# Scan step sizes made beside the grouped heads' values, differential values 512 columns wide

## The chip, the core and the metric

The kernel runs on one core of a Trainium2 chip as one program. The metric is the device time of one execution in microseconds; a run's time is that of its one core. TensorE (PE in the profile) multiplies, VectorE (DVE) and ScalarE (ACT) do the elementwise work, GpSimd (POOL) and SyncE (SP) issue transfers from their own queues. Matmuls accumulate into PSUM, eight banks of 512 float32 columns on each of 128 partitions.

## The reference, cut to what matters

Two layers of a hybrid trunk over 256 context tokens and 256 latent tokens of 1024 channels. In each layer one input projection feeds a bidirectional state-space scan, grouped-query attention (8 query heads, 2 heads of keys and values) and differential attention (8 heads); a gated merge, a layer norm and a gated feed-forward follow. Three parts of that projection matter here, with their widths:

```
p = split(h @ w_in)        # h: 512 tokens x 1024 channels
dt = softplus(p.dt + dt_bias)          # 64 columns: step sizes, 32 heads in 2 directions
a_dt = dt * -exp(a_log)                # decays of the scan, summed along the tokens
v_gqa  = p.gv                          # 256 columns: values of the 2 grouped heads
v_diff = p.dv                          # 1024 columns: values of the 8 differential heads, 128 each
o_head = softmax(...) @ v_head         # both attentions
```

## The kernel before

The program is not written in the order in which it runs. `trunk` records every operation in a plan; `Plan.schedule` (a list scheduler, `round` at line 346) then orders the operations of all engines at once, from a priority, a price for each operation (`cost`, line 208) and the room in SBUF and PSUM, and emits that order. So each instruction's place follows from the whole plan, every instruction has the same source line (586; 585 in the changed kernel), and the trace is read by tile names: `w` holds weights, `s` and `shared` are 2 KB work tiles (whole or shared by smaller ones), `ps` a PSUM bank, `cst` and `id` constants.

Every large product is exact float32 made from three reduced-precision terms: an operand is cast to float32r (`wh`, on ScalarE) and the rest is subtracted (`wl`, on VectorE); `mm3` (line 692) multiplies high by high, high by low and low by high into one bank:

```
T.matmul(ps, ah, bh, start=start, stop=False)
T.matmul(ps, ah, bl, start=False, stop=False)
T.matmul(ps, al, bh, start=False, stop=stop)
```

`proj` (line 931) makes 128 output channels of the projection with `dense`: weights stationary, the tokens `xT` moving, 8 channel blocks x 3 terms = 24 matmuls of 512 tokens. The first `HALVES` = 7 products of a layer over all tokens are cut into two halves of 256 tokens (context, latent), 48 matmuls, so that the context half can begin before the latent tokens are ready. In layer 0 some products begin when only half of the channels is modulated (`early_terms`, line 883).

Values are made the other way round, tokens on the partitions: the tokens are stationary, the weights move. `values` (line 1174) makes 256 columns for the 4 blocks of 128 tokens, two blocks to a PSUM bank one after the other: 4 x 8 x 3 = 96 matmuls of 256 columns. It is called once a layer for the grouped heads (`O_GV`, within `gqa_steps`, after the first key head) and four times for the differential heads (`O_DV`, `diff_steps`, one call for two heads).

The step sizes (`do_dt`, line 952) are a `proj` of 64 columns. Their softplus is computed with heads on the partitions, context in the upper and latent tokens in the lower half; four transposes bring steps and decays to tokens on partitions; matmuls with triangular constants make the running sums that the scan (`ssm_steps`) reads.

The scan's stream is interleaved with the attention and merge streams (`side`) by recorded TensorE cost: `advance` moves `side` on by `RATIO[i]` = 1.52 or 1.42 times what the scan's steps brought. Weights come in loads of 512 KB through SP's queue into 15 slots. Products with many terms take a bank from a share of six of the eight (`psd`, `CAP["d"]`).

## Time and profile before

| | |
|---|---|
| median of 3 runs | 2346.48 us (2346.24 to 2348.11) |
| the profiled execution, first to last instruction | 2345.3 us |
| TensorE busy | 2301.0 us, 98% |
| VectorE, ScalarE busy | 1670.1 us (71%), 1422.4 us (61%) |
| TensorE's mean granted clock | 0.993 |

The profiled execution's own span is 1.2 us under the median of the runs. Busy time of TensorE is a union of modelled spans, so the pace of a kind of matmul is read below from the start of one run of equal matmuls to the start of what follows.

### The profile page before, as it was taken

The numbers are of one execution on the slowest core, as the hardware profiler recorded it, in microseconds if no ns is written. First come the engines' busy times: TensorE is split into PE (matmuls) and PEld (weight loads), VectorE is DVE, ScalarE is ACT, GpSimd is POOL, SyncE is SP. The second block draws the span as 40 slices with busy tenths as digits, with TensorE's granted clock in tenths as the row PEclk, the third lists the DMA queues.
The fourth block names the chain that finished last, engine by engine and source line by source line (L and its number), as shares of the span: only waits on it lengthen the run. The fifth ranks groups of instructions, "written<-read, shape, count | busy, mean of one in ns | idle before, by whom it ended". The sixth has DMA issues, their size and how long they took to land. (4 is left out here: it accounts for less than half of the span.)

```text
span 2345.3 us, 38903 instructions
## 1 busy us (share of the span) xinstructions
PE 2301.0 (98%) x14423; PEld 1940.3 (83%) x14423; DVE 1670.1 (71%) x3438; ACT 1422.4 (61%) x2887; POOL 135.1 (6%) x216
## 2 busy tenths in 40 slices
PE   8999999999999999999999999999999999999998
PEld 4877777887887788898777778989988798998997
DVE  3889857888988864476333337999698888767655
ACT  4778745867767753345323235888586676646554
POOL 3102102000100100000000000001010100000000
PEclk9999999999999999999999999999999999999998
DMA  9746544332433465576555425527443345798662
GB/s 332 214 135 175 181 132 135 102 112 72 133 104 98 133 216 175 184 219 213 171 163 168 139 74 151 150 76 217 132 129 114 105 126 164 214 274 240 191 188 66
DMA packets 520702, 370.37 MB, mean 158 GB/s; under 512 B 20706, under 2 KB 472674, under 8 KB 520512
## 3 DMA queue, kind: packets, MB, share of 16 engines
q1 hardware_dynamic: 507296, 329.63, 47.3%
q0 software_dynamic: 13216, 38.25, 5.5%
q8 instruction: 113, 1.85, 0.3%
q14 instruction: 77, 0.63, 0.1%
HBM read 334.00 MB, written 33.82 MB: 157 GB/s over the span
## 5 line engine op out<-in xcount | busy, mean ns | idle before, releaser
L586 PE MATMUL ps<-s,w 128*128 128x512 f32 (+2 forms) x7608 | 1524.0, 355 | 8.2 <-DVE s L586 4.6
L586 PEld LDWEIGHTS ps<-s,w 128*128 128x128 f32 (+1 forms) x7608 | 1236.0, 189 | 237.1 <-issue 28.8
L586 ACT CAST w<-w 128x1024 fp32r<-128x1024 f32 (+2 forms) x486 | 454.4, 944 | 486.3 <-DVE w L586 256.8
L586 DVE TENSOR_TENSOR w<-w,w 128x1024 fp32r<-128x1024 f32 (+2 forms) x486 | 528.0, 1092 | 299.8 <-PE ps L586 203.0
L586 PE MATMUL ps<-shared,w 128*128 128x256 f32 x2544 | 313.2, 283 | 0.0
L586 PE MATMUL ps<-s,s 128*64 128x128 f32 (+6 forms) x2320 | 303.2, 361 | 7.6 <-DVE s L586 2.1
L586 PEld LDWEIGHTS ps<-shared,w 128*128 128x128 f32 x2544 | 308.5, 192 | 0.5 <-issue 0.3
L586 ACT ACTIVATE s<-s 128x512 f32<-128x512 f32 x424 | 260.6, 630 | 31.0 <-DVE s L586 24.7
L586 PEld LDWEIGHTS ps<-s,s 128*64 128x64 f32 (+3 forms) x2320 | 186.9, 152 | 90.6 <-issue 31.9
L586 DVE TENSOR_TENSOR s<-s,s 128x512 f32<-128x512 f32 (+2 forms) x298 | 196.2, 674 | 36.7 <-ACT s L586 34.5
L586 DVE TENSOR_TENSOR s<-s,ps 128x512 f32<-128x512 f32 x116 | 79.1, 684 | 133.3 <-PE ps L586 65.7
L586 DVE SCALAR_TENSOR_TENSOR s<-ps,misc,s 128x510 f32<-128x510 f32 (+2 forms) x188 | 139.3, 741 | 13.9 <-ACT s L586 11.8
L586 PE MATMUL ps<-w,s 128*128 128x256 f32 x960 | 119.7, 284 | 0.0
L586 PEld LDWEIGHTS ps<-w,s 128*128 128x128 f32 x960 | 117.2, 192 | 2.2 <-issue 1.5
L586 DVE TENSOR_TENSOR shared<-shared,shared 128x256 f32<-128x256 f32 (+2 forms) x241 | 97.2, 417 | 24.4 <-ACT shared L586 22.6
L586 DVE TENSOR_TENSOR s<-ps,s 128x256 fp32r<-128x256 f32 (+1 forms) x204 | 85.6, 444 | 30.4 <-ACT s L586 25.7
L586 ACT ACTIVATE shared<-shared 128x256 f32<-128x256 f32 x232 | 92.4, 416 | 23.4 <-DVE shared L586 20.7
L586 ACT CAST s<-ps 128x256 fp32r<-128x256 f32 (+1 forms) x204 | 74.4, 396 | 36.0 <-PE ps L586 32.1
L586 ACT ACTIVATE s<-ps,misc 128x512 f32<-128x512 f32 x68 | 50.6, 744 | 73.2 <-PE ps L586 73.0
L586 POOL DMA_DIRECT2D s<-dram x96 | 71.9, 753 | 375.0 <-PE ps L586 274.7
L586 ACT ACTIVATE s<-ps,tiny 128x512 f32<-128x512 f32 x112 | 76.7, 689 | 26.5 <-DVE tiny L586 18.9
L586 DVE SCALAR_TENSOR_TENSOR shared<-ps,misc,shared 128x256 f32<-128x256 f32 (+2 forms) x144 | 67.2, 478 | 29.4 <-PE ps L586 20.4
(102 smaller groups left out, 1512.5 us busy)
## 6 DMA issues: line engine op xcount, KB each, us to landing
w<-in_w_in_dram SPq DMA_DIRECT2D x200, 512.0 KB, 4.0
s<-in_ada_w_dram SPq DMA_DIRECT2D x192, 256.0 KB, 4.9
w<-in_ffn_w_in_dram SPq DMA_DIRECT2D x88, 512.0 KB, 3.9
s<-dram POOLq DMA_DIRECT2D x96, 256.0 KB, 5.6
s<-dram SPq DMA_DIRECT2D x64, 256.0 KB, 4.1
w<-in_w_ssm_out_dram SPq DMA_DIRECT2D x32, 512.0 KB, 4.1
w<-in_ffn_w_out_dram SPq DMA_DIRECT2D x32, 512.0 KB, 3.9
shared<-dram SPq DMA_DIRECT2D x112, 128.0 KB, 3.9
```

The lines of the kernel that those rows point to most:

```text
L586: getattr(attr[op.eng], fn)(*[real(v) for v in args], **{a: real(v) for a, v in kw.items()})
```

## The change

The 64 step-size columns are appended to the 256 columns of the grouped heads' values: `shared_values` moves 320 columns past each stationary token block, one bank for each of the 4 token blocks. These values are recorded ahead of all streams of a layer (in layer 0 their first half within `early_terms`), and `do_dt` reads columns 256 to 320 of the four banks, tokens already on partitions; its own projection, the copies into halves and the four transposes are gone, and bias and decay are loaded as rows broadcast to all partitions. `values` makes 512 columns (four heads) in a call for the differential heads, twice a layer, one bank a token block. `value_terms` goes through the channels two blocks at a time and, for each pair, through all four banks, which stay open until the last pair. The planner's price of a float32r matmul is now columns / 2.4 + m / 9.6 ns, m being the stationary operand's columns; it was max(columns / 2.4, 107) + 2.5 ns. Lines that only lose a comment are left out here.

```diff
-                return max(n / 2.4 if n >= 256 else 4 * n / 2.4, 107) + 2.5
+                return (n if n >= 256 else 4 * n) / 2.4 + m / 9.6
...
     def load_scalars(i):
-        na = tiny(2)
-        for r in (0, 64):
-            G.dma_start(out=na[r:r + 64, 0:1], in_=a_log[i].rearrange("t h -> (t h)").unsqueeze(1))
-            G.dma_start(out=na[r:r + 64, 1:2], in_=dt_bias[i].rearrange("t h -> (t h)").unsqueeze(1))
-        A.activation(na[:, 0:1], na[:, 0:1], AF.Exp)
+        na = th().rearrange("p (a c) -> p a c", c=64)
+        for m, src in enumerate((a_log, dt_bias)):
+            G.dma_start(out=na[:, m, :], in_=src[i].rearrange("t h -> (t h)").unsqueeze(0).to_broadcast([128, 64]))
+        A.activation(na[:, 0, :], na[:, 0, :], AF.Exp)
+        V.tensor_scalar(na[:, 0, :], na[:, 0, :], -1.0, None, ALU.mult)
...
-    def value_terms(pss, ws, blocks=range(4), have=()):
-        for t in blocks:
-            o = pss[t // 2][:, (t % 2) * 256:(t % 2) * 256 + 256]
-            ts_ = slice(t * 128, t * 128 + 128)
-            for k0, (wh, wl) in ws.items():
-                if k0 == 0 and t in have:
-                    continue
-                for k in range(k0, k0 + 4):
-                    mm3(o, xT[k][0][:, ts_], xT[k][1][:, ts_], wh[:, k - k0, :], wl[:, k - k0, :],
-                        k == 0, k == KT - 1)
+        n = sum(a.shape[-1] for a in src)
+        raw = plan.tile("w4", [128, len(ks), n], F32, "raw", CAP["raw"])
+        c = 0
+        for a in src:
+            w = a.shape[-1]
+            rows = a[ks[0] * 128:(ks[-1] + 1) * 128].rearrange("(k p) c -> p k c", p=128)
+            S.dma_start(out=raw[:, :, c:c + w], in_=rows)
+            c += w
+        wh = plan.tile("w4", [128, len(ks), n], F32R, "wh", CAP["wh"])
+        wl = plan.tile("w4", [128, len(ks), n], F32R, "wl", CAP["wl"])
+        A.copy(wh, raw)
+        V.tensor_sub(wl, raw, wh.bitcast(F32))
+        return wh, wl
+    def value_terms(pss, src, k0, k1):
+        n = sum(a.shape[-1] for a in src)
+            wh, wl = load_values(src, (k, k + 1))
+            for t in range(4):
+                ts_ = slice(t * 128, t * 128 + 128)
+                for d in range(2):
+                    mm3(pss[t][:, 0:n], xT[k + d][0][:, ts_], xT[k + d][1][:, ts_], wh[:, d, :], wl[:, d, :],
+                        k + d == 0, k + d == KT - 1)
     def load_x(q):
...
+    def shared_values(W):
+        return [W[:, O_GV:O_GV + 256], W[:, O_DT:O_DT + 64]]
     def early_terms():
...
-        for key in EARLY:
-            if key == O_GV:
-                w = load_w(W[0:512, key:key + 256], 4, 256)
-                early[0, key] = ([psd(), psd()], w)
-                value_terms(early[0, key][0], {0: w}, (0, 2))
-            else:
-                cols = 64 if key == O_DT else 128
-                w = load_w(W[:, key:key + cols], KT, cols, 32 if key == O_GK else 0)
-                early[0, key] = (psd(), w)
-                dense(early[0, key][0][0:cols], w, KT, xcols(0, NT), cols=cols, ks=range(4))
+        early[0, O_GV] = [psd() for _ in range(4)]
+        value_terms(early[0, O_GV], shared_values(W), 0, 4)
+        w = load_w(W[:, O_GK:O_GK + 128], KT, 128, 32)
+        early[0, O_GK] = (psd(), w)
+        dense(early[0, O_GK][0], w, KT, xcols(0, NT), ks=range(4))
...
-        def do_dt():
-            ps = proj(O_DT, 0, cols=64)
-            xx, e, z, pl = [t1() for _ in range(4)]
-            for r in range(2):
-                A.copy(xx[64 * r:64 * r + 64], ps[0:64, 256 * r:256 * r + 256])
-            V.tensor_scalar(xx, xx, nega[i][:, 1:2], None, ALU.add)
+        def do_dt(raw):
+            e, z, pl, lg = [t1() for _ in range(4)]
+            xx = fl(dt_tok)
+            for cc in range(4):
+                V.tensor_tensor(dt_tok[:, cc, :], raw[cc][:, 256:320], nega[i][:, 1, :], ALU.add)
...
-            V.tensor_scalar(xx, xx, 0.0, None, ALU.max)
+            V.tensor_scalar(lg, xx, 0.0, None, ALU.max)
...
-            V.tensor_scalar(pl, xx, nega[i][:, 0:1], -1.0, ALU.mult, ALU.mult)
-            ps2 = psum()
-            for t in range(2):
-                s = slice(t * 128, (t + 1) * 128)
-                transpose(ps2[:, t * 128:t * 128 + 128], pl[:, s])
-                transpose(ps2[:, 256 + t * 128:384 + t * 128], xx[:, s])
-            by_half = lambda a: a.rearrange("p (t r c) -> p r t c", r=2, c=64)
-            V.tensor_copy(adt_tok.rearrange("p (r t) c -> p r t c", r=2), by_half(ps2[:, 0:256]))
-            A.copy(dt_tok.rearrange("p (r t) c -> p r t c", r=2), by_half(ps2[:, 256:512]))
+            V.scalar_tensor_tensor(xx, pl, 2.0, lg, ALU.mult, ALU.add)
+            V.tensor_tensor(adt_tok, dt_tok, nega[i][:, 0, :].unsqueeze(1).to_broadcast([128, 4, 64]), ALU.mult)
             ps3 = psum()
...
         def ssm_steps():
-            do_dt()
...
-        def values(col):
-            ws = lambda k0: load_w(W[k0 * 128:(k0 + 4) * 128, col:col + 256], 4, 256)
-            if (i, col) in early:
-                pss, w = early.pop((i, col))
-                value_terms(pss, {0: w, 4: ws(4)}, have=(0, 2))
-            else:
-                pss = [psd(), psd()]
-                value_terms(pss, {0: ws(0), 4: ws(4)})
+        def values(src, cols):
+            n = sum(a.shape[-1] for a in src)
+            pss, k0 = early.pop((i, O_GV), None) if cols == 256 else None, 4
+            if pss is None:
+                pss, k0 = [psd() for _ in range(4)], 0
+            value_terms(pss, src, k0, KT)
             out = []
             for ps in pss:
-                vh, vl = t2(512, F32R), t2(512, F32R)
-                split(vh, vl, ps)
-                out.append((vh, vl))
-            return out
+                out.append((t2(cols, F32R), t2(cols, F32R)))
+                split(*out[-1], ps[:, 0:cols])
+            return out, pss
         def pt_tiles(nk):
...
             for kt in range(n):
-                vh, vl = v[kt // 2]
-                ks = slice((kt % 2) * 256 + e * 128, (kt % 2) * 256 + e * 128 + 128)
+                vh, vl = v[kt]
+                ks = slice(e * 128, e * 128 + 128)
...
-                if hd % 2 == 0:
-                    v = values(O_DV + hd * 128)
+                if hd % 4 == 0:
+                    v, _ = values([W[:, O_DV + hd * 128:O_DV + hd * 128 + 512]], 512)
...
                 normed(ps, NT, C_KN, kh, kl)
-                if e == 0:
-                    v = values(O_GV)
...
-                        ps = pv_mm(v, e, pt, nk)
+                        ps = pv_mm(gv, e, pt, nk)
...
+        gv, raw_dt = values(shared_values(W), 256)
+        do_dt(raw_dt)
```

Counted over the whole program, TensorE loses 960 matmuls of 256 columns (weights moving) and all 72 of the step-size product (24 of 512, 48 of 256) and gains 192 of 320 and 384 of 512; eight transposes go; since the step sizes no longer take one of the seven cut products of layer 1, one more product is cut there (48 of 256 for 24 of 512). Otherwise the kinds of work are the same, and the planner has ordered everything anew. Three places, as the built programs have them:

TensorE at the first block of differential values in layer 0; `ps_4769` and `ps_4724` are the first banks of that block, `w` the moving weights, `s` the stationary tokens. Before, the bank's first token block takes all 24 terms, then its second begins (the last row):

```order
L586 MATMUL ps_4708<-s_46_547,w_937_4641 128x512
L586 MATMUL ps_4769<-w_944_4270,s_32_317 128x256
L586 MATMUL ps_4769<-w_945_4655,s_32_317 128x256
L586 MATMUL ps_4769<-w_944_4270,s_33_322 128x256
...
L586 MATMUL ps_4769<-w_947_4397,s_47_556 128x256
L586 MATMUL ps_4769<-w_944_4270,s_32_317 128x256
```

After, six terms go to each of four banks, and the first bank's next six begin with the last row:

```order
L585 MATMUL ps_4663<-s_46_575,w_944_4621 128x512
L585 MATMUL ps_4724<-w_953_4233,s_32_270 128x512
...
L585 MATMUL ps_4724<-w_953_4233,s_35_314 128x512
L585 MATMUL ps_4740<-w_953_4233,s_32_270 128x512
...
L585 MATMUL ps_4740<-w_953_4233,s_35_314 128x512
L585 MATMUL ps_4756<-w_953_4233,s_32_270 128x512
...
L585 MATMUL ps_4756<-w_953_4233,s_35_314 128x512
L585 MATMUL ps_4768<-w_953_4233,s_32_270 128x512
...
L585 MATMUL ps_4768<-w_953_4233,s_35_314 128x512
L585 MATMUL ps_4724<-w_956_4370,s_36_356 128x512
```

What moved: a bank was complete after 48 matmuls in a row and the next was then opened; now four banks are opened within 19 matmuls and are complete only at the end of the block's 96.

TensorE from layer 0 to layer 1, before; the first row is the last of the feed-forward product that the layer norm of the latent tokens waits for, `64x256` are step sizes, `ps_14207` the first key head, `ps_14262` grouped values, `cst` rows the layer norm:

```order
L586 MATMUL ps_14166<-s_2635_13729,w_2740_14209 128x256
L586 MATMUL ps_14207<-s_2646_14105,w_2788_14066 128x256
...
L586 MATMUL ps_14185<-s_2640_14077,w_2777_14232 64x256
...
L586 MATMUL ps_14262<-w_2800_14141,s_2640_14077 128x256
...
L586 MATMUL ps_14262<-w_2803_14158,s_2654_14134 128x256
L586 MATMUL ps_14323<-shared_37_14318,cst_271 32x256
...
L586 MATMUL ps_14346<-shared_37_14318,cst_271 128x256
L586 MATMUL ps_14185<-s_2640_14077,w_2776_14044 64x256
...
L586 MATMUL ps_14207<-s_2640_14077,w_2788_14066 128x256
L586 MATMUL ps_14207<-s_2640_14077,w_2789_14250 128x256
```

And after, where `128x320` are values and step sizes together, and `ps_14197` the first key head:

```order
L585 MATMUL ps_13920<-s_2642_13460,w_2747_13932 128x256
...
L585 MATMUL ps_13937<-w_2788_13948,s_2647_13799 128x320
...
L585 MATMUL ps_13943<-w_2796_13885,s_2659_13843 128x320
L585 MATMUL ps_14030<-shared_7_11237,cst_295 32x256
...
L585 MATMUL ps_13943<-w_2796_13885,s_2662_13895 128x320
L585 MATMUL ps_14062<-shared_31_12051,cst_295 128x256
L585 MATMUL ps_14087<-w_2787_13789,s_2647_13799 128x320
...
L585 MATMUL ps_14104<-w_2787_13789,s_2647_13799 128x320
...
L585 MATMUL ps_14197<-s_2647_13799,w_2817_13914 128x256
```

What moved: context halves of step sizes and keys stood beside the grouped values ahead of the layer norm's last matmul (`128x256` with `cst`); now only the values with step sizes do, and the keys follow them all.

SP's queue in layer 0's first stretch, before (rows that would repeat are left out):

```order
L586 DMA s_49_165<-in_ctx_dram 128x512
L586 DMA w_69_167<-in_w_in_dram 128x8x64
L586 DMA w_73_171<-in_w_in_dram 128x8x128
L586 DMA w_77_177<-in_w_in_dram 128x4x256
L586 DMA s_83_181<-in_ada_w_dram 128x512
...
L586 DMA s_105_259<-in_x_dram 128x512
L586 DMA cst_271<-in_consts_dram 128x1408
L586 DMA w_170_280<-in_w_in_dram 128x4x256
L586 DMA dram_289<-s_138_226 128x2x256
```

After:

```order
L585 DMA s_51_161<-in_x_dram 128x512
L585 DMA w_73_167<-in_w_in_dram 128x2x64
L585 DMA w_73_167<-in_w_in_dram 128x2x256
...
L585 DMA w_79_178<-in_w_in_dram 128x8x128
L585 DMA s_84_181<-in_ada_w_dram 128x512
...
L585 DMA cst_295<-in_consts_dram 128x1408
L585 DMA w_157_301<-in_w_in_dram 128x2x256
L585 DMA w_157_301<-in_w_in_dram 128x2x64
L585 DMA w_160_317<-in_w_in_dram 128x2x256
L585 DMA w_160_317<-in_w_in_dram 128x2x64
L585 DMA w_180_335<-in_w_in_dram 128x8x128
```

What moved: one load of step-size weights for all channels and two of 4 channel blocks for the values have become pairs of loads (256 and 64 columns) for two channel blocks; two projection weights follow straight behind the last pair, ahead of the modulation weights.

## Rows read from the trace of the kernel before

**Rows 1.** The page of before: busy time, and the granted clock in 40 slices.

```profile
PE 2301.0 (98%) x14423; PEld 1940.3 (83%) x14423; DVE 1670.1 (71%) x3438; ACT 1422.4 (61%) x2887; POOL 135.1 (6%) x216
...
PEclk9999999999999999999999999999999999999998
```

**Rows 2.** Who TensorE waited for, whole span: us in total, times, longest.

```profile
PE ps L586 <- ACT shared L586: 10.7, 11, 2.3
PE ps L586 <- DVE s L586: 9.9, 9, 2.9
PE ps L586 <- ACT s L586: 7.6, 9, 2.8
...
PE ps L586 <- DVE tiny L586: 0.2, 1, 0.2
```

**Rows 3.** Busy time by stage; last three columns granted clock, DMA share, GB/s.

```profile
45.00:75.00 30.00, 28.82 (x204) 23.99 (x205) 23.67 (x58) 20.78 (x40) 0.53 (x1) 0.94 1.07 322
...
430.00:700.00 270.00, 265.78 (x1577) 216.16 (x1576) 229.66 (x551) 191.51 (x451) 21.38 (x34) 1.00 0.36 104
...
800.00:1450.00 650.00, 650.00 (x3430) 534.46 (x3426) 335.06 (x516) 271.89 (x402) 2.95 (x5) 1.00 0.55 168
```

**Rows 4.** Groups of TensorE instructions, shapes apart: count, busy us, mean ns, idle.

```profile
L586 PE MATMUL ps<-w,s 128*128 128x256 f32 x960 | 119.7, 284 | 0.0
...
L586 PE MATMUL ps<-s,w 128*64 128x512 f32 x24 | 9.6, 528 | 4.6 <-DVE s L586 4.6
```

**Rows 5.** TensorE by time: start us, us, operation, count [idle before]; a values block, layer 0.

```profile
424.78 5.38 PE L586 MATMUL ps<-s,w 128*128 128x512 f32 x23
430.00 11.68 PE L586 MATMUL ps<-w,s 128*128 128x256 f32 x96
441.51 5.63 PE L586 MATMUL ps<-s,w 128*128 128x512 f32 x24
...
449.83 0.96 PE L586 MATMUL ps<-s,s 64*128 64x512 f32 x4 [0.65 <-ACT shared L586]
```

**Rows 6.** TensorE in order of time, the start of layer 0.

```profile
26.49 1.54 PE L586 MATMUL ps<-s,w 128*64 128x512 f32 x3 [2.87 <-DVE s L586]
...
35.87 3.03 PE L586 MATMUL ps<-w,s 128*128 128x256 f32 x24
...
46.18 2.82 PE L586 MATMUL ps<-s,w 128*64 128x512 f32 x6 [1.70 <-DVE s L586]
...
54.99 7.99 PE L586 MATMUL ps<-w,s 128*128 128x256 f32 x62
62.90 1.92 PE L586 MATMUL ps<-s,s 128*32 128x512 f32 x16
64.76 4.82 PE L586 MATMUL ps<-s,w 128*128 128x256 f32 x38
```

**Rows 7.** VectorE in order of time, same stretch: a weight's low part is made.

```profile
56.47 1.16 DVE L586 TENSOR_TENSOR w<-w,w 128x1024 fp32r<-128x1024 f32 x1
```

**Rows 8.** TensorE in order of time, from layer 0 to layer 1.

```profile
1453.60 0.52 PE L586 MATMUL ps<-w,s 128*128 128x256 f32 x3
...
1455.58 1.84 PE L586 MATMUL ps<-w,s 128*128 128x256 f32 x14
...
1459.65 0.70 PE L586 MATMUL ps<-shared,cst 128*128 128x256 f32 x2 [0.63 <-ACT shared L586]
1463.18 7.36 PE L586 MATMUL ps<-s,w 128*64 128x256 f32 x48 [2.83 <-ACT s L586]
1470.38 1.96 PE L586 MATMUL ps<-w,s 128*128 128x256 f32 x15
```

**Rows 9.** Busy time and granted clock there.

```profile
1460.00:1470.00 10.00, 7.17 (x47) 6.48 (x46) 8.76 (x22) 8.28 (x20) 0.00 (x0) 0.83 0.31 105
```

**Rows 10.** Busy time within two blocks of differential values (columns as in rows 3).

```profile
430.00:441.40 11.40, 11.40 (x97) 11.40 (x96) 7.62 (x15) 9.57 (x21) 0.00 (x0) 1.00 0.18 47
508.50:520.00 11.50, 11.50 (x97) 11.49 (x96) 6.28 (x12) 5.77 (x12) 0.00 (x0) 1.00 0.24 68
```

More of the change, by code (lines that the diff above doesn't have):

```diff
@@ L42 @@
 RATIO = (1.52, 1.42)
-EARLY = (O_DT, O_GK, O_GV)
 HALVES, HALVES_FF = 7, 2
@@ L838, in xcols, with load_values @@
         return lambda k: (xT[k][0][:, a:b], xT[k][1][:, a:b])
-    def value_terms(pss, ws, blocks=range(4), have=()):
-        for t in blocks:
-            o = pss[t // 2][:, (t % 2) * 256:(t % 2) * 256 + 256]
-            ts_ = slice(t * 128, t * 128 + 128)
-            for k0, (wh, wl) in ws.items():
-                if k0 == 0 and t in have:
-                    continue
-                for k in range(k0, k0 + 4):
-                    mm3(o, xT[k][0][:, ts_], xT[k][1][:, ts_], wh[:, k - k0, :], wl[:, k - k0, :],
-                        k == 0, k == KT - 1)
+    def load_values(src, ks):
+        n = sum(a.shape[-1] for a in src)
[13 more added lines that the diff above has]
+        n = sum(a.shape[-1] for a in src)
+        for k in range(k0, k1, 2):
+            wh, wl = load_values(src, (k, k + 1))
[4 more added lines that the diff above has]
+                        k + d == 0, k + d == KT - 1)
     def load_x(q):
@@ L969, in do_dt @@
             V.scalar_tensor_tensor(pl, pl, 1.0, z, ALU.add, ALU.mult)
-            V.scalar_tensor_tensor(xx, pl, 2.0, xx, ALU.mult, ALU.add)
-            V.tensor_scalar(pl, xx, nega[i][:, 0:1], -1.0, ALU.mult, ALU.mult)
-            ps2 = psum()
-            for t in range(2):
-                s = slice(t * 128, (t + 1) * 128)
-                transpose(ps2[:, t * 128:t * 128 + 128], pl[:, s])
-                transpose(ps2[:, 256 + t * 128:384 + t * 128], xx[:, s])
-            by_half = lambda a: a.rearrange("p (t r c) -> p r t c", r=2, c=64)
-            V.tensor_copy(adt_tok.rearrange("p (r t) c -> p r t c", r=2), by_half(ps2[:, 0:256]))
-            A.copy(dt_tok.rearrange("p (r t) c -> p r t c", r=2), by_half(ps2[:, 256:512]))
+            V.scalar_tensor_tensor(xx, pl, 2.0, lg, ALU.mult, ALU.add)
+            V.tensor_tensor(adt_tok, dt_tok, nega[i][:, 0, :].unsqueeze(1).to_broadcast([128, 4, 64]), ALU.mult)
             ps3 = psum()
@@ L1250, in diff_steps @@
                             yield
-                    ps = pv_mm(v, hd % 2, pt, nk)
+                    ps = pv_mm(v, hd % 4, pt, nk)
                     sq = t1()
```

## The prediction

> **What bounds the kernel now.** I read the page first: TensorE is busy in 98% of the span, 2301.0 of 2345.3 us, and its granted clock is full in nearly every slice [rows 1]. Then the waits: what TensorE waits for is short and scattered. The answer has nine releasers, from 10.7 us down to 0.2; the first three make 28.2 us in 29 waits [rows 2], and all nine 38.6 us. So the end is set by the sum of TensorE's work, and a part of the change is worth what it takes from that sum, unless it makes a new wait. The table by stage shows where a new wait could arise [rows 3]. At 45 to 75 us transfers are at a share of 1.07, so work that comes earlier there may find its weights missing. In the mixed stage at 430 to 700 us VectorE is busy 229.66 of 270 us, 85%: near enough to a second bound that work withheld from it can come back as a wait. In the feed-forward, 800 to 1450 us, TensorE never idles.
>
> **The prices.** A busy share is no pace, so I take starts. In a clean stretch 23 matmuls of 512 columns run from 424.78 to 430.00 us, 227.0 ns each; 96 with 256 columns, weights moving, from 430.00 to 441.51, 119.9 ns each [rows 5]. Twice the columns thus cost 227.0 and not 239.8: each matmul carries about 13 ns besides its columns. The Trainium skill, "TensorE: Matmul & The Clock Gate", section Back-to-back issue gap, gives an isolated matmul columns / 2.4 + 2.5 ns, which would be 109.2 and 215.8 ns. By that rule a pair merged into one would save 2.6 ns instead of 12.8, the differential values 1.0 us in all, and the time would be about 2340; both rows speak against it, and the rows decide. Matmuls of 320 columns don't occur before. They lie between 119.9 and 227.0 ns; by columns, on the line between these rows, 146.7. I take that, since 320 is nearest to 256.
>
> **The change part by part.**
>
> *Differential values.* Of the 960 matmuls with weights moving [rows 4], 192 are the grouped values' (96 a layer) and 768 the differential ones. 768 x 119.9 ns = 92.1 us become 384 x 227.0 ns = 87.2 us: -4.9 us. The elements cast, split and loaded stay the same, so nothing is added on the other engines; SP issues ten loads more in the whole program, the values' pairs.
>
> *Grouped values with step sizes.* Before, 96 x 119.9 ns = 11.5 us a layer, and the step sizes: in layer 0 24 matmuls of 512 columns, at 227.0 ns 5.4 us (the group's mean is far longer [rows 4], since these lie in the start's waits and low clock); in layer 1 48 of 256, 5.8 us. After, 96 x 146.7 ns = 14.1 us a layer. Layer 0: 16.9 to 14.1, -2.8 us; layer 1: 17.3 to 14.1, -3.2 us. At the ends of the unknown price, 11.5 or 21.8 us a layer, the two layers together would give -11.2 or +9.4 instead of -6.0.
>
> *Transposes.* Eight of 128 columns go. At most 119.9 ns each, by the nearest row; I take 0.1 us, -0.8 us. That the step sizes' chain is shorter, and their bias and decay now come as broadcast rows on POOL's queue, I cost at nothing: TensorE has other products to run while the chain runs, as it has now behind 46.18 us [rows 6]; without that cover a late row would hold the scan and nothing else.
>
> *One more product cut in layer 1.* 48 x 119.9 - 24 x 227.0 ns = +0.3 us.
>
> TensorE's work in all: -4.9 - 2.8 - 3.2 - 0.8 + 0.3 = **-11.4 us**.
>
> *The start of layer 0.* TensorE waits for the modulated first half until 26.49 us and for the second until 46.18, is then busy without a gap, and reaches the next projection product at 64.76 [rows 6]. Early work lies under the wait that ends at 46.18; only what follows it shortens the end. Before, 12 + 12 of step sizes and key head and 72 of values follow: 2.7 + 2.7 + 8.6 = 14.0 us. After, 48 of 320 and 12 of 512: 9.8 us, since the early half now covers all four blocks. That is 4.2 us sooner, not 2.8. But the next product then stands at about 46.2 + 9.8 = 56.0 us, and before, its weight's low part was done at 56.47 + 1.16 = 57.6 us [rows 7]; with the transfers as full as they are and two more issues ahead of it, I count 1.4 us as lost there, which leaves -2.8. Four banks for values, one for keys and one for modulation leave two for the transposes of the second half of the tokens, where three were free; a copy waits for a bank: 0 to 1 us, I take **+0.5**.
>
> *From layer 0 to layer 1.* The layer norm of the latent tokens is a chain that TensorE covers with work on context tokens. From the order, 24 step-size, 24 key and 19 value matmuls lie ahead of its last sum: 67 x 119.9 ns = 8.0 us; after, 48 x 146.7 = 7.0 us. Before, TensorE still waited 0.63 and 2.83 us there, and began again at 1463.18 [rows 8], and after that idle time the granted clock stood for a part of those 10 us at the lower of its two levels, 1.2 instead of 2.4 GHz, a mean of 0.83 [rows 9]. With 1 us less cover and the chain as long, the wait grows by as much, less what the reordered queue gives: 0 to 1.5, I take **+0.8**. VectorE takes splits of context values between the chain's steps, in work that it has either way.
>
> *The planner.* A dearer matmul changes priorities and the interleave by `RATIO`. No row prices that. What it could gain is the short waits outside the start, the layer norms and the end, an estimated quarter of the 38.6 us, 9 us; what it could lose may be as much. I take 0 and keep +-9.
>
> Sum: 2345.3 - 11.4 + 0.5 + 0.8 = 2335.2 us of span. The median of the runs is 1.2 us above this execution, so **2336.4 us**.
>
> **The rivals.**
>
> *A, slower: four open banks starve VectorE.* In a block of values now, VectorE falls from 85% to 7.62 of 11.40 and 6.28 of 11.50 us [rows 10]: nothing else fills banks that it could read. TensorE's wait behind such a block is so far 0.65 us [rows 5]. A block becomes 21.8 us long with four of eight banks held to its last matmul. If VectorE has nothing in the second half, 0.85 x 10.9 = 9.3 us of its work is put off, four times, where the stage's slack is 15%. Where 4 us a block come back as waits, the time is 2336.4 + 16 = 2352. It is slower than before once a block costs 10.1 / 4 = 2.5 us. Against it: total time in such blocks falls from 92.1 to 87.2 us, and the deficit of a block now is followed by almost no wait. The Trainium skill, "Perfetto Trace Analysis", section Optimizing Tensor Performance, asks that independent groups rotate through banks so that emptying one overlaps filling the next; holding four to the end goes against that. By that rule the rival would come true; the small wait after a block now is what this trace says of it. Chance 0.12.
>
> *B, the start gives nothing.* Transfers, at a share of 1.07, set the pace to 75 us [rows 3], so the 2.8 us of layer 0 are waited for anyway, and the border costs its 1.5: 2336.4 + 2.8 + 0.7 = 2340. For it speak the share and the low part at 57.6; against it that TensorE has no gap after 46.18 [rows 6]. Chance 0.13.
>
> *C, wide value matmuls don't run at the pace of the wide products*, whose weights stand still: at 239.8 ns the differential values save nothing, 2341. Against it: with 256 columns the weights' place makes no such difference, 119.9 ns with weights moving [rows 5] and 127 at most with weights standing, 38 in 4.82 us [rows 6]. Chance 0.03.
>
> *D, the planner's price, now near the measured paces, removes half or more of the loose waits:* 2336.4 - 7 = 2329. Chance 0.10.
>
> *The forecast:* 2336.4, its own range 2332 to 2341. Chance 0.62.
>
> **How the numbers follow.** The forecast, B and C lie below 2341.8 (a change of 0.2%, about what this kernel's measurements can tell from none) for the most part, D wholly: 0.57 + 0.10 + 0.02 + 0.10 = 0.79 faster. The upper edge of the forecast, B and C and the mild half of A: 0.14 same. The strong half of A: 0.07 slower. The range reaches from D's middle to A's mild half, 2328 to 2345; some 0.08 lie beyond either end, from A, and from a 320-column price or a planner's gain better than taken.
>
> **What would show it.** Starts in blocks of 512 with weights moving should be 227 ns apart, of 320 about 147. The block of values should be 21.8 us long, and the wait behind it under 1.5 us; longer, with VectorE under half busy in the block's second half, A holds. The next projection product behind values and modulation in layer 0 should start at about 58 us instead of 64.76; a gap ahead of it is B. The wait at the layers' border should be 3 to 4.5 us. TensorE's busy time should fall to about 2290 us, with waits near 40. The prediction is wrong if waits grow by over 6 us, wherever the planner put them.

## The result, and the profile after

The changed kernel takes 2372.48 us, the median of four runs (2370.5 to 2376.45), against 2346.36 us before (2344.41 to 2348.11): a ratio of 1.0113, with a 95% interval of 1.0098 to 1.0127. It is 26 us slower, where 2336.4 was forecast. The profiled execution spans 2370.7 us.

The page of the changed kernel, the lines that answer to [rows 1]:

```profile
PE 2305.7 (97%) x13983; PEld 1917.8 (81%) x13983; DVE 1674.8 (71%) x3450; ACT 1419.7 (60%) x2887; POOL 132.9 (6%) x212
...
PEclk9999999999999999999999999999999999999999
```

TensorE has 440 matmuls fewer and is busy for 4.7 us more. Two things make a busy time longer without work: a lower clock, and waits too short to show, since the ends of matmuls are modelled. The waits that do show, over the whole span (us in total, times, longest), as in [rows 2]:

```profile
PE ps L585 <- ACT s L585: 17.8, 16, 3.1
PE ps L585 <- ACT shared L585: 16.3, 19, 2.1
PE ps L585 <- DVE s L585: 12.1, 20, 1.3
...
PE ps L585 <- DVE tiny L585: 3.1, 4, 1.1
```

All releasers add up to 58.5 us, against 38.6. The new waits are many and short, for ScalarE first of all. Where they lie is seen in the table by stage (columns as in [rows 3]), here of the changed kernel:

```profile
45.00:75.00 30.00, 30.00 (x213) 26.49 (x213) 26.62 (x66) 23.21 (x46) 0.55 (x1) 0.94 1.07 329
75.00:200.00 125.00, 116.81 (x746) 92.56 (x746) 105.79 (x272) 90.01 (x222) 15.43 (x23) 1.00 0.48 143
200.00:300.00 100.00, 95.81 (x539) 72.93 (x538) 78.18 (x191) 74.02 (x167) 15.31 (x23) 0.98 0.59 178
430.00:700.00 270.00, 260.41 (x1358) 202.53 (x1357) 227.34 (x552) 190.58 (x450) 20.05 (x32) 0.99 0.37 106
700.00:850.00 150.00, 143.38 (x770) 109.87 (x769) 124.50 (x282) 102.98 (x229) 9.43 (x14) 0.98 0.40 119
850.00:1400.00 550.00, 549.95 (x2769) 446.71 (x2768) 260.70 (x365) 211.97 (x295) 2.20 (x4) 1.00 0.56 174
```

The same stretches of the kernel before, those that [rows 3] doesn't hold:

```profile
75.00:200.00 125.00, 122.47 (x802) 98.52 (x801) 108.52 (x276) 96.82 (x231) 15.43 (x23) 1.00 0.51 149
200.00:300.00 100.00, 100.00 (x570) 79.07 (x569) 84.56 (x202) 76.30 (x176) 15.01 (x23) 1.00 0.62 188
700.00:850.00 150.00, 149.13 (x811) 117.23 (x810) 123.19 (x274) 106.25 (x225) 8.18 (x12) 1.00 0.45 135
```

Read downward: the start is now full (30.00 of 30), the feed-forward loses nothing, and four stretches of layer 0 in which the two streams are mixed lose some: 5.7, 4.2, 5.4 and 5.8 us of busy time (from 300 to 430 us TensorE is busy throughout in both kernels). The first two of these lie ahead of the first block of differential values, which stands at 437 us. So waits behind that block cannot be their cause.

What one such loss looks like is seen at 200 us, in the timeline of the changed kernel (start, us, engine; in brackets the idle time ahead and what ended it), and in the window behind it:

```profile
200.18 0.33 SPq L585 DMA_DIRECT2D s<-dram  x1
...
208.86 0.62 ACT L585 CAST s<-s 128x512 fp32r<-128x512 f32 x1 [3.21 <-DMA s<-dram]
...
210.34 0.94 DVE L585 SCALAR_TENSOR_TENSOR s<-shared,shared,s 128x128 f32<-128x128 f32 x3 [2.79 <-ACT s L585]
...
212.56 1.22 PE L585 MATMUL ps<-s,s 128*128 128x256 f32 x4 [2.93 <-ACT s L585]
...
213.58 1.05 PE L585 MATMUL ps<-s,w 128*128 128x512 f32 x2
```

```profile
213.00:217.00 4.00, 4.00 (x32) 3.18 (x32) 3.02 (x9) 3.98 (x11) 1.11 (x2) 0.63 0.76 231
```

ScalarE is idle for 3.21 us ahead of a cast whose row was asked for at 200.18 and is there 8.6 us later; what ScalarE runs behind the cast ends a wait of VectorE (2.79 us) and one of TensorE (2.93 us). TensorE then works at a mean granted clock of 0.63: after the wait a part of the stretch is at the lower level, 1.2 GHz. The four matmuls of 256 columns there take 1.02 us to the next start, 255 ns each, about twice the 120 ns of the full clock. Between 50 and 2320 us the trace has 20.5 us at the lower level, against 10.2 before; at that pace the difference cost an estimated 5 us.

A measure that leaves the modelled ends out is used below as **the rest**. I add up, over all matmuls, the time from each start to the next, less columns / 2.4 + weight columns / 9.6 ns, which is 226.7, 146.7 and 120.0 ns for the three kinds of value matmul. The priced part goes from 2222.2 to 2211.2 us, 11.0 less; the rest goes from 114.2 to 151.5 us, 37.3 more. That is the whole result. The growth lies in the mixed stages of both layers. From the first projection product behind the start (64.76 us before, 53.15 after) to the layer norm at the border (1459.65, 1475.24) the rest goes from 38.1 to 69.0 us; from the work behind that border (1463.18, 1485.24) to the first feed-forward transfer of layer 1 (2099.7, 2128.6) it goes from 38.7 to 49.8.

### The profile page after: what moved, and what is told of

Same layout as the page of the kernel before. It is cut to its first block, busy times and chain, and to the rows that moved or that the text cites. A ratio compares the mean times of both kernels' runs of the same rounds, so it can differ in the third digit from the quotient of the medians.

```text
span 2370.7 us, 38113 instructions
## 1 busy us (share of the span) xinstructions
PE 2305.7 (97%) x13983; PEld 1917.8 (81%) x13983; DVE 1674.8 (71%) x3450; ACT 1419.7 (60%) x2887; POOL 132.9 (6%) x212
## 4 chain that ended last, share of the span: by engine, by line
PE 72%; DVE 10%; ACT 8%; DMA 5%; issue 4%; POOL 0%; SPq 0%; POOLq 0%; DVEq 0%; ACTq 0%
PE ps L585 72%; DVE s L585 5%; ACT s L585 4%; ACT shared L585 3%; DVE shared L585 2%; DVE w L585 1%; DVE tiny L585 1%; DMA s<-dram 1%; ACT w L585 1%; DMA s<-in_ada_w_dram 1%; DMA shared<-dram 1%; DMA dram<-shared 1%; DMA w<-in_w_in_dram 0%; DMA s<-in_x_dram 0%; SPq L585 0%
## 5 line engine op out<-in xcount | busy, mean ns | idle before, releaser
L585 PE MATMUL ps<-s,w 128*128 128x512 f32 (+1 forms) x7560 | 1508.7, 355 | 2.7 <-ACT s L585 1.3
L585 PEld LDWEIGHTS ps<-s,w 128*128 128x128 f32 x7560 | 1227.6, 189 | 231.3 <-issue 33.5
L585 ACT CAST w<-w 128x1024 fp32r<-128x1024 f32 (+3 forms) x488 | 455.0, 941 | 540.4 <-DVE w L585 331.6
L585 DVE TENSOR_TENSOR w<-w,w 128x1024 fp32r<-128x1024 f32 (+3 forms) x488 | 528.7, 1088 | 302.9 <-PE ps L585 184.3
L585 PE MATMUL ps<-s,s 128*64 128x128 f32 (+6 forms) x2080 | 269.6, 370 | 21.0 <-DVE s L585 6.6
L585 PEld LDWEIGHTS ps<-s,s 128*64 128x64 f32 (+3 forms) x2080 | 153.2, 150 | 99.9 <-issue 26.9
L585 DVE SCALAR_TENSOR_TENSOR s<-ps,misc,s 128x508 f32<-128x508 f32 (+2 forms) x188 | 139.5, 742 | 14.7 <-ACT s L585 12.3
L585 PE MATMUL ps<-w,s 128*128 128x512 f32 (+1 forms) x576 | 122.9, 372 | 3.4 <-ACT s L585 3.1
L585 ACT ACTIVATE shared<-shared 128x256 f32<-128x256 f32 (+1 forms) x234 | 93.5, 416 | 23.1 <-DVE shared L585 19.7
L585 DVE TENSOR_REDUCE tiny<-ps 128x1 f32<-128x512 f32 (+1 forms) x144 | 81.5, 592 | 3.1 <-PE ps L585 3.0
```

The costliest lines, as they stand in the source:

```text
L585: getattr(attr[op.eng], fn)(*[real(v) for v in args], **{a: real(v) for a, v in kw.items()})
```

## The experiments

Theory P: the planner's new price of a matmul, which changes nothing that runs but its order, put the work in a worse order. Theory W, rival A of the prediction: the wide block with its four open banks makes the engines wait in any order. Theory O: any new order costs or gives some ten us by luck. Ratios are to the kernel before, run beside each.

### Which part of the change

**e1**, the changed kernel at the old price:

```diff
-                return (n if n >= 256 else 4 * n) / 2.4 + m / 9.6
+                return max(n / 2.4 if n >= 256 else 4 * n / 2.4, 107) + 2.5
```

> The changed kernel with one line undone: the planner prices a matmul as the kernel before did (256 columns 109 ns, 512 columns 216 ns) and no longer at the 120.0 and 226.7 ns that the trace shows. The matmuls, copies and transfers that run are the same; only their order can differ. Theory P (the new price puts the work in a worse order): 2335 to 2345 us, the forecast that the work alone gave. Theory O (every new list order of this program costs or gives some ten us, whichever edit made the planner draw it): anywhere from 2345 to 2380. Theory W (the four banks that stay open in the 512-column block, or the new start of a layer, make the engines wait whatever the order): 2365 to 2380, as the changed kernel.

2346.43 us, ratio 0.9994 (0.9985 to 1.0004). One line that no engine executes takes 26 us away.

**e2**, the kernel before with the same line the other way round.

> The kernel before with one line of the change: the planner's price of a matmul. The work that runs is the same as before. Theory P: some 20 to 35 us slower, 2366 to 2381, with new waits of TensorE for ScalarE in the mixed stages. Theory O: a new order, within 20 us either way of 2346. Theory W: 2346 within 5, since neither the wide block nor the new start of a layer is in it.

2383.89 us, ratio 1.0165 (1.0143 to 1.0186): 36 us slower with the work of before. P has the sign and about the size of both runs, which lie 1.4 and 2.9 us beyond its ranges. W has neither, and in e2 O's 20 us are passed too; e1 by itself lies within O's wide range.

**e3**, the changed kernel with narrow differential values:

```diff
...
-                if hd % 4 == 0:
-                    v, _ = values([W[:, O_DV + hd * 128:O_DV + hd * 128 + 512]], 512)
+                if hd % 2 == 0:
+                    v = values2(O_DV + hd * 128)
...
```

`values2`, left out here, makes 256 columns, two token blocks to a bank, as before.

> The changed kernel with the differential values as they were: 256 columns wide, for two heads at a time, two token blocks to a bank, two banks. The merged step sizes and grouped values and the new price stay. It gives back 4.9 us of TensorE work. Theory W with the wide block as the cause: the waits behind it go, 2340 to 2355. Theory O: the lost time is scattered and not tied to the block, so a re-drawn order lands anywhere from 2350 to 2390. Theory P: 2372 plus 5, near 2377.

2368.28 us, ratio 1.0089 (1.0074 to 1.0104). The loss stays, 13 us above W's range, so the block is not its main cause. P had foretold 2377, 9 us more; O's range holds it.

**e4**, the kernel before with wide differential values alone. In it heads 2 and 3 of each four read the values of heads 0 and 1.

```diff
...
-                if hd % 2 == 0:
-                    v = values(O_DV + hd * 128)
+                if hd % 4 == 0:
+                    v = wide_values(O_DV + hd * 128)
...
```

`wide_values`, left out here, makes 512 columns with four open banks.

> The kernel before with only the differential values made 512 columns wide with four banks open, one block for four heads; the step sizes, the grouped values and the planner's price stay as before. It saves 4.9 us of TensorE work. Theory W: 10 to 25 us slower than before, with TensorE waiting after each wide block. Theory O: 2341 plus or minus some 15, with waits away from the blocks. Theory P: 2341 within 4.

2351.17 us, ratio 1.0014 (1.0005 to 1.0023): 3.6 us slower, with 5 us less work. That is under W's 10 to 25 us and 6 above P's range; O's holds it. Together with e3 this looks like 9 us of waits that go with the block; e17 and e18 come back to that.

e1 also leaves a question: it has all of the saved work, and is no faster than before. Its last layer norm shows a good part of it. TensorE, then busy time and clock, in e1:

```profile
2125.11 1.22 PE L585 MATMUL ps<-shared,cst 128*128 128x256 f32 x2 [6.09 <-DVE shared L585]
```

```profile
2120.00:2130.00 10.00, 4.89 (x25) 2.33 (x29) 7.42 (x16) 3.73 (x9) 0.00 (x0) 0.55 1.00 318
2130.00:2145.00 15.00, 12.62 (x78) 11.25 (x71) 9.51 (x26) 7.77 (x17) 0.00 (x0) 0.73 0.05 15
```

And in the kernel before:

```profile
2125.92 0.70 PE L586 MATMUL ps<-shared,cst 128*128 128x256 f32 x2 [2.73 <-DVE shared L586]
```

The norm's sum starts 0.8 us sooner than before, but after a wait of 6.09 and not 2.73 us, and a clock of 0.55 and 0.73 follows. From the first feed-forward transfer of layer 1 (at 2094.9 us, 4.8 sooner than before) to the end, the rest is 22.0 us, where it was 15.6. Of the 11 us of saved work, these 4.8 were left by then: in layer 0's mixed stages, from 60 us to 829, the rest is 55.4 us, where it was 44.1, in short waits with no one place. Here the last of the saving went.

### Through what the price acts

The planner adds up 1597 us for VectorE and 1288 for ScalarE; the trace has 1675 and 1420. They are priced 5 and 9% low. The old price made TensorE's planned sum 2116 us, low as well; the new one makes it 2239. Theory L: what counts is the level of TensorE's price against the others' too low ones, since the planner then believes that VectorE and ScalarE have time in hand. Theory S: it is the new proportion of wide to narrow. Theory X: it is the mixing of the two streams by `RATIO`, which counts in priced TensorE work.

**e5**, the new price at 0.945 of its level:

```diff
+                return 0.945 * ((n if n >= 256 else 4 * n) / 2.4 + m / 9.6)
```

> The changed kernel with the new price of a matmul times 0.945 in the planner, so that TensorE's planned work comes to 2131 us in place of 2239 (it was 2116 at the old price). The proportions of the new price between wide and narrow matmuls stay. Theory L (what costs the time is the level: in the plan VectorE's instructions add up to 1597 us and ScalarE's to 1288, in the trace to 1675 and 1420, so that at the dearer TensorE price the planner thinks that the other two have time that they don't have): 2338 to 2352. Theory S (the new proportions between wide and narrow matmuls): 2365 to 2380. Theory O (any new order, drawn at random): anywhere from 2340 to 2385.

2336.56 us, ratio 0.995 (0.9934 to 0.9967). With the work of the change, the proportions of its price, and the level near the old one, the time is that of the forecast, 1.4 us under L's range and 11 us better than the kernel before it ran beside (2348.07). O's range begins 3 us above it. S is out for the changed kernel.

**e6**, the full new price, and the others dearer:

```diff
-            dur = self.cost(eng, fn, outs[0], ins, kw)
+            dur = self.cost(eng, fn, outs[0], ins, kw) * {"Act": 1.10, "DVE": 1.05}.get(eng, 1.0)
```

> The changed kernel with its new price, and in the planner ScalarE's instructions 10% and VectorE's 5% dearer, so that their sums in the plan (1417 and 1677 us) are those of the trace (1420 and 1675). Theory L: the balance between the engines is as in the plan of before again, 2338 to 2355. Theory S: 2365 to 2380. Theory O: anywhere from 2340 to 2385.

2352.01 us, ratio 1.0013 (1.0004 to 1.0022): 20 of the 26 us come back without touching TensorE's price. That is what L says of the balance; O's range holds it too.

**e7**, the new price in the planner's clock, the old one in `spent`, by which the streams are mixed:

```diff
             self.spent["PE"] += dur
+            if not more and fn != "transpose" and ins[1].dt() == F32R:
+                n, m = self.free(ins[1]), ins[0].shape[-1]
+                self.spent["PE"] += max(n / 2.4 if n >= 256 else 4 * n / 2.4, 107) + 2.5 - dur
```

> The changed kernel with the new price in the planner's clock, but the old price in the account by which the two streams are mixed (so many microseconds of side work for each of the state-space stream). Theory L, and S: the mixing has little to do with it, 2360 to 2380. Theory X (the new price shifted the mixing of the two streams away from what the ratios were set for): 2338 to 2352. Theory O: anywhere from 2340 to 2385.

2359.58 us, ratio 1.0048 (1.0033 to 1.0063): 13 us faster than the changed kernel, just below L's range and well above X's. The mixing may have a share; one order can't say, as e13 and e14 show.

**e8**, as e1 with the ratio of layer 0 at 1.54 (`RATIO = (1.54, 1.42)`).

> The changed kernel with the old price (as in the first run of these) and the ratio of side work to state-space work in layer 0 at 1.54 in place of 1.52; the same matmuls, copies and transfers as in the changed kernel. In the first run the 11 us of saved work were eaten by 7 us at the last layer norm of layer 1 (a wait of 6.1 us and a slow clock behind it) and by scattered short waits. Theory O for this rest: another order has other short waits, and 2335 to 2350 is all possible, with 2336 if the wait at that layer norm is as short as before. Theory W (four open banks and the new start cost a fixed 8 to 11 us whatever the order): 2344 to 2350.

2343.41 us, ratio 0.9983 (0.9972 to 0.9995). Another order at the same price gives 3 us, not clear of the noise, since the two intervals overlap; its wait at the last layer norm is as long (6.4 us).

**e9 and e10**, the new price at 0.97 and 0.90.

> The changed kernel with the new price times 0.97 (TensorE's planned work 2180 us, between the 2131 us that ran in 2336.6 and the 2239 us that ran in 2372.5). Theory L, as a straight line between those two: 2353, taken as 2345 to 2360. Theory O (the times of single orders are luck): anywhere from 2336 to 2385, with no relation to the level.

> The changed kernel with the new price times 0.90 (TensorE's planned work 2042 us). Theory L: TensorE is already cheap enough at 0.945 for the others to be sent ahead of it, so there is little more to win: 2332 to 2346. Theory O: anywhere from 2336 to 2385.

2354.1 us (ratio 1.0034, 1.0021 to 1.0047) and 2344.11 (0.9988, 0.9978 to 0.9997). At 0.97 the time lies on L's line; at 0.90 nothing more is won.

**e11**, the kernel before with the new price at 0.945, and **e12**, the changed kernel with the old price at 1.05.

> The kernel before with the proportions of the new price, times 0.945 (TensorE's planned work 2142 us; 2123 at the old price, which ran in 2347.6, and 2251 at the new price alone, which ran in 2383.9). Theory L: 2340 to 2356, no more than the old price gives, since the work is that of before. Theory O: anywhere from 2340 to 2390.

> The changed kernel with the old price times 1.05 (TensorE's planned work 2208 us in the old proportions; 2116 at the old price itself, which ran in 2346.4). Theory L: slower than that, 2353 to 2372 by the line through the levels of the new price. Theory S (it is the new proportions that hurt): 2340 to 2350. Theory O: anywhere from 2340 to 2385.

e11 takes 2361.51 us, ratio 1.0064 (1.0049 to 1.0079): 22 us better than e2, but 5.5 above L's range and 14 above before. e12 takes 2351.93, ratio 1.002 (1.001 to 1.0029): slower than e1 by 5.5 us, where L wanted at least 7. That lies between S's range and L's. The sign is L's in both; the sizes are not. In e11 the planned sum is close to that of the old price (2142 and 2123): on the line through 2131 and 2239 us the difference would cost an estimated 6 us of the 14. The new proportions or a worse draw could each have made the others, and no other order of the kernel before was run to tell. So orders at one level differ too, and it had to be seen by how much.

### Level against luck

**e13 to e16**: two more orders at the full price and two at 0.945, drawn by `RATIO = (1.50, 1.42)` and `(1.54, 1.42)`.

> The changed kernel with its new price as it is, and the ratio of side work to state-space work in layer 0 at 1.50 in place of 1.52: the same work, another order at the same level of the price. Theory L (the level of TensorE's price against the other engines' decides): 2360 to 2385. Theory O (each order has its own luck, some 15 us either way): anywhere from 2335 to 2385.

> As the run before, with the ratio at 1.54. Theory L: 2360 to 2385. Theory O: anywhere from 2335 to 2385.

> The changed kernel with the new price times 0.945, which ran in 2336.6, and the ratio in layer 0 at 1.50: the same work, another order at that level. Theory L: 2332 to 2348, all below the runs at the full new price. Theory O: anywhere from 2335 to 2385.

> As the run before, with the ratio at 1.54. Theory L: 2332 to 2348. Theory O: anywhere from 2335 to 2385.

At the full price 2374.95 us (ratio 1.0116, 1.0099 to 1.0133) and 2363.62 (1.007, 1.0055 to 1.0085); at 0.945 2343.31 (0.9984, 0.9974 to 0.9993) and 2335.74 (0.9949, 0.9935 to 0.9964). Three orders at the full price take 2363.6 to 2375.0, three at 0.945 take 2335.7 to 2343.3. They don't meet. Take all orders of the changed kernel with its wide block, but for e6 and e7, where something else in the planner was altered too: the six planned at 2131 us or less (e1, e5, e8, e10, e15, e16) take 2335.7 to 2346.4, the two at 2180 and 2208 (e9, e12) 2354.1 and 2351.9, the three at 2239 take 2363.6 to 2375.0. Luck would hardly sort them so; O falls as the cause of the 26 us.

**e17 and e18**: narrow differential values, as in e3, at 0.945, with the ratio at 1.52 and 1.54.

> The changed kernel with the differential values 256 columns wide and two banks open, as in the kernel before, and the new price times 0.945, ratio 1.52 (with the wide values this ran in 2336.6). It has 5 us more TensorE work. Theory N (the wide block costs nothing beyond its own work once the order is right): 2338 to 2346. Theory W (the four open banks cost some 9 us of waits in any order, as the two runs on the block alone suggest: 4 us faster without it at the full price, 4 us slower with it alone at the old one): 2328 to 2335.

> As the run before, with the ratio at 1.54 (with the wide values 2335.7). Theory N: 2337 to 2345. Theory W: 2327 to 2334.

2361.91 us (ratio 1.0058, 1.0045 to 1.0071) and 2344.25 (0.9983, 0.9974 to 0.9992). W is out in both: without the wide block the kernel is slower, by 25 and by 8.5 us. e18 fits N; e17 is 16 us above it, and shows that a good level does not make every order good.

The planned work and the rest are in us; the rest is that of the profiled execution.

| run | differential values | price | planned TensorE work | median | rest |
|---|---|---|---|---|---|
| before | narrow | old | 2123 | 2346.4 | 114.2 |
| after | wide | new | 2239 | 2372.5 | 151.5 |
| e1 | wide | old | 2116 | 2346.4 | 126.4 |
| e2 | narrow (kernel before) | new | 2251 | 2383.9 | 151.2 |
| e11 | narrow (kernel before) | new x 0.945 | 2142 | 2361.5 | 127.2 |
| e3 | narrow | new | 2244 | 2368.3 | 144.5 |
| e17 | narrow | new x 0.945 | 2136 | 2361.9 | 137.6 |
| e13 | wide, ratio 1.50 | new | 2239 | 2375.0 | 156.6 |
| e15 | wide, ratio 1.50 | new x 0.945 | 2131 | 2343.3 | 124.4 |
| e14 | wide, ratio 1.54 | new | 2239 | 2363.6 | 143.8 |
| e16 | wide, ratio 1.54 | new x 0.945 | 2131 | 2335.7 | 115.5 |
| e5 | wide | new x 0.945 | 2131 | 2336.6 | 115.3 |
| e18 | narrow, ratio 1.54 | new x 0.945 | 2136 | 2344.3 | 116.2 |
| e8 | wide, ratio 1.54 | old | 2116 | 2343.4 | 118.1 |
| e10 | wide | new x 0.90 | 2042 | 2344.1 | 122.5 |
| e9 | wide | new x 0.97 | 2180 | 2354.1 | 128.4 |
| e12 | wide | old x 1.05 | 2208 | 2351.9 | 129.4 |

Five pairs differ in the level alone: after and e5, e13 and e15, e14 and e16, e3 and e17, e2 and e11. The cheaper TensorE is faster in all five, by 35.9, 31.6, 27.9, 6.4 and 22.4 us.

The profile of e5 shows what the level does. TensorE's waits over its whole span:

```profile
PE ps L585 <- ACT shared L585: 12.5, 14, 2.2
PE ps L585 <- DVE s L585: 8.4, 12, 1.3
PE ps L585 <- ACT s L585: 5.8, 8, 2.8
```

And its stages:

```profile
75.00:200.00 125.00, 122.32 (x785) 95.23 (x784) 106.67 (x284) 94.08 (x231) 17.50 (x26) 0.99 0.52 145
200.00:300.00 100.00, 99.03 (x538) 76.47 (x538) 78.46 (x186) 72.49 (x161) 13.25 (x20) 1.00 0.67 200
430.00:700.00 270.00, 264.97 (x1404) 206.25 (x1402) 228.67 (x551) 193.25 (x449) 20.63 (x33) 1.00 0.36 104
700.00:850.00 150.00, 149.50 (x794) 116.61 (x795) 124.60 (x273) 104.63 (x224) 8.91 (x13) 1.00 0.47 139
```

The busy time of the mixed stages is back, and so is the clock at 700 to 850. VectorE's own waits tell which engine is ahead. In the changed kernel:

```profile
DVE w L585 <- PE ps L585: 184.3, 138, 4.3
DVE s L585 <- ACT s L585: 161.3, 152, 3.4
```

In e5:

```profile
DVE w L585 <- PE ps L585: 215.8, 151, 4.3
DVE s L585 <- ACT s L585: 138.3, 129, 4.9
```

With TensorE cheap in the plan, VectorE's weight splits wait 31.5 us more for TensorE, and its work on `s` tiles 23.0 us less for ScalarE. Only the second of these is seen in all five pairs. The first falls by 6.0 and 9.2 us from e13 to e15 and from e14 to e16, and rises by 28.8 and 9.4 from e3 to e17 and from e2 to e11. The second, at the full price in e13, e14, e3 and e2:

```profile
DVE s L585 <- ACT s L585: 161.7, 147, 3.2
DVE s L585 <- ACT s L585: 155.5, 145, 3.3
DVE s L585 <- ACT s L585: 163.5, 149, 3.6
DVE s L586 <- ACT s L586: 164.9, 146, 3.2
```

And at 0.945, in e15, e16, e17 and e11:

```profile
DVE s L585 <- ACT s L585: 150.6, 152, 3.7
DVE s L585 <- ACT s L585: 146.2, 137, 4.9
DVE s L585 <- ACT s L585: 148.7, 143, 3.3
DVE s L586 <- ACT s L586: 149.1, 149, 4.2
```

So ScalarE, whose price is the furthest below its busy time, holds VectorE up less at the cheaper TensorE. That both engines then run further ahead of TensorE, and that what the plan doesn't know, such as a row that is 8.6 us on its way, finds a reserve there, is an argument from these waits and not shown.

## Why the prediction was wrong

The step that failed is the planner's: "A dearer matmul changes priorities and the interleave by `RATIO`. No row prices that. [...] I take 0 and keep +-9." It cost 26 us (e1 against the changed kernel), and 28 to 36 against 0.945 of the price, in three orders of the changed kernel. The bound of 9 was worked out from the waits that were there to be won; nothing bounds from above what an order can lose. The planner's source and the page together held the warning: its sums for VectorE and ScalarE lie 4 and 9% under the busy times in [rows 1], and raising TensorE's alone moves that balance. Rival D, by which a price near the measured paces removes waits, had the sign wrong.

Point by point:

**The prices were right.** In the changed kernel's first wide block in layer 0, TensorE by time, with busy time in its two halves:

```profile
437.55 21.92 PE L585 MATMUL ps<-w,s 128*128 128x512 f32 x96
459.31 11.04 PE L585 MATMUL ps<-s,w 128*128 128x512 f32 x48
```

```profile
437.55:448.50 10.95, 10.95 (x50) 9.07 (x49) 7.50 (x18) 8.92 (x17) 0.00 (x0) 1.00 0.34 93
448.50:459.40 10.90, 10.90 (x50) 9.03 (x49) 6.89 (x8) 3.96 (x6) 0.00 (x0) 1.00 0.36 100
```

Start to start, (459.31 - 437.55) / 96 = 226.7 ns; 227 was foretold. Rival C is out. By the Trainium skill, "TensorE: Matmul & The Clock Gate", section Back-to-back issue gap, an isolated matmul of 512 columns would take 215.8 ns; those of this block, each with a weight load of its own, take 11 ns more. That rule is the planner's old price, so the price that is further from the trace gave the better order here.

**Rival A did not happen here.** VectorE is busy for 6.89 of 10.90 us in the second half, 63%, and no wait follows the block, nor the two whole blocks of layer 1 (1714.29 and 1851.29 us). Without the wide block e17 and e18 are slower, not faster. The Trainium skill, "Perfetto Trace Analysis", section Optimizing Tensor Performance, asks that groups rotate through banks; the trace of this block bears no wait out for holding four of them.

**The start and the border.** TensorE in time, the start and the border of the changed kernel:

```profile
42.87 1.14 PE L585 MATMUL ps<-s,w 128*128 128x512 f32 x3 [1.09 <-DVE s L585]
43.96 0.85 PE L585 MATMUL ps<-w,s 128*128 128x320 f32 x4
...
45.05 8.26 PE L585 MATMUL ps<-w,s 128*128 128x320 f32 x44
53.15 5.08 PE L585 MATMUL ps<-s,w 128*128 128x256 f32 x41
```

```profile
1473.04 2.37 PE L585 MATMUL ps<-w,s 128*128 128x320 f32 x15
1475.24 0.59 PE L585 MATMUL ps<-shared,cst 128*128 128x256 f32 x2
...
1485.24 9.02 PE L585 MATMUL ps<-w,s 128*128 128x320 f32 x48 [3.11 <-ACT s L585]
```

Fifteen matmuls of 320 columns take 2.20 us, 146.7 ns each, as taken. The next projection product starts at 53.15 us; about 58 was foretold, and 64.76 was before. No gap precedes it, so rival B is out, and the 1.4 us that I counted as lost to transfers were not. The second half's work resumes at 42.87 instead of 46.18, which I had not foreseen. At the border the wait is 3.11 us; 3 to 4.5 was foretold.

**The work** fell by 11.0 us in priced matmuls; 11.4 was foretold. TensorE's busy time rose all the same, to 2305.7 us, where 2290 was foretold. **Its worth** as time depends on the order: 10 us of it are seen in e5 and e16 (2336.6 and 2335.7), none in e1. The last test in the prediction, "wrong if waits grow by over 6 us, wherever the planner put them", is what came true: 58.5 against 38.6 us.

**What stays open.** At one level, orders still lie up to 26 us apart (e16 and e17, with 5 us of work between them), and I have no reading of an order that would tell a good one ahead of its run. How much of the loss is the mixing (e7) is open too. That the level of TensorE's price against the others' made the loss of the changed kernel is shown by e5, e6 and the times in the order of the planned sums; how the level acts on the chip is argued from the waits. That late rows matter was seen in the one wait at 200 us, and not tried. In the kernel before the level explains less (e11), and its own order may be a good draw: all three edits of that kernel (e2, e4, e11) lost, and no second order of it at its own price was run.

## What to carry to other kernels

A cost table in a planner is read as a set: here the plan got worse when one engine's price was made true and the others stayed too low, so compare the plan's sum for each engine with its busy time on the page before touching one price. Test a change that feeds a planner in two runs, the work alone and the price alone; here the first was no slower than before (e1), and the second 36 us slower (e2). And price a re-ordering by what it can lose, with a few orders of the same work, never at 0.

## What was unexpected of the hardware

A short wait cost more than its length: after 2.93 us without work for TensorE the granted clock was 0.63 from 213 to 217 us, after only 1.27 us (ahead of 542.59 us) it was 0.52 from 543.5 to 547 us, and at the 6.09 us of e1's last layer norm it was 0.55 from 2120 to 2130 us, the end of the wait among them, and 0.73 over the 15 us behind. A row asked for on SP's queue at 200.18 us, with the DMA share at 0.93 from 200 to 209 us, took 8.6 us to arrive.
